# TensorE operands at chosen positions within a 64-byte line of SBUF, in a two-layer decoder trunk

## The chip, the cores and the metric

The kernel runs on one core of a Trainium2 chip. The metric is the device time of one execution in microseconds, lower is better.

## The reference

The input x has 256 positions of 1024 float32 values. Two layers follow each other; each is a token mixer and a feed-forward block, both on a root-mean-square norm of the running x and added to it.

- Layer 0's mixer is a short gated convolution: h times a 1024 x 3072 matrix gives three parts b, c and v; a causal convolution of width 3 over positions runs over c times v; the result times b goes through a 1024 x 1024 matrix.
- Layer 1's mixer is attention with 16 heads of 64 and rotary positions, causal over the 256 positions (one block, so the block selection selects nothing), with projections q, k, v and o.
- The feed-forward block of each layer goes up to 2 x 2816 columns, runs a causal width-3 convolution over positions, takes silu of one half times the other half, and goes down to 1024.

```python
x = x + short_conv_mixer(h, w_in, w_conv, w_out)      # layer 0
x = x + moba_attention(h, w_qkv, w_o)                 # layer 1
x = x + (silu(g) * u) @ w_down    # [g|u] = causal_dwconv(h @ w_up, w_conv), in both layers
```

A last norm gives the output.

## The kernel before

Everything is kept transposed, channels on the 128 partitions and positions along the free axis, so an activation tile is 128 x 256 float32. Each float32 operand of a product is split in two float32r tiles, a high part (the value rounded) and a low part (what is left). A product is then three matmuls, in `passes`: high weights with high inputs, high weights with low inputs, low weights with high inputs. Weights of 128 x 128 are the stationary operand and 256 columns of input the moving one, except in two places. In the v projection (`v_stage`) and in the down projection of layer 1 (`TokenAccum`) the inputs are stationary and 512 columns of weights move past them.

Weights are streamed in units of 128 x 1024 float32. A list made when the kernel is built, `PLAN`, has all units in the order of their use. `load_chunk` issues the DMAs of two units into a tile raw, four of which are in flight. `split_next` takes the next unit, makes its high tile hi on ScalarE and its low tile lo on VectorE, into rings of six tiles each. `unit(key)` hands out the pair and splits up to it if that has not been done. `slot` is called between groups of matmuls: it splits one or more units ahead and runs one step of each task that is waiting (evacuations, convolutions, softmax). The order on each engine is the order in which the code issues the instructions; the class `InOrder` pins it.

The stages of the program, in order, with the names that the profile's rows use:

- `FIRST`, the units of the first two column blocks of layer 0's input projection, in an order that follows x's arrival, and then "in", the rest of it. Outputs are cv and b, inputs xh and xl.
- "out", which sums up the mixer's output projection in PSUM over all its inputs (class `Accum`), between the "in" units. Output mo, inputs ys..h and ys..l.
- "up" and "down" of layer 0. Outputs gu and fo; inputs of up are xh and xl, of down ps_..h and ps_..l. Down is again an `Accum`.
- "q", "k" and "v" of layer 1 (outputs qk and v), the scores s, the transposes pt of the probabilities, the values o, and the output projection "o" (output ao, inputs oh and ol).
- "up" and "down" of layer 1, the latter a `TokenAccum`, and the last norm.

`scaled` makes xh and xl from x and the norm's gain; `split_tiles` gives the tiles for ys and ps; `values` those for oh and ol. `finish_norm` makes rms and rstd, each 260 columns wide. All instructions go through the call in `InOrder`, so the profile names line 92 for nearly all of them and rows are told apart by tile names.

Where a tile lies. SBUF tiles of a pool lie one behind the other, in the order of their first use, each beginning at a multiple of 32 bytes per partition. Three kinds of small tile are no multiple of 64 bytes long: eps and table (one column, 4 bytes, that take up 32), rms and rstd (1040 bytes, 1056 with the filling). Everything behind one of them is shifted by 32 bytes against a 64-byte line. The positions that come of this, as bytes past a multiple of 64:

| Stage (output) | Stationary operand | Moving operand |
|---|---|---|
| first, in (cv, b) | weights 32 | inputs 0 |
| out (mo) | weights 32 | inputs 32 |
| up of layer 0 (gu) | weights 32 | inputs 0 |
| down of layer 0 (fo) | weights 32 | inputs 32 |
| q, k (qk) | weights 32 | inputs 0 |
| v (v) | inputs 0 | weights 32 |
| o (ao) | weights 32 | inputs 32 |
| up of layer 1 (gu) | weights 32 | inputs 0 |
| down of layer 1 (fo) | inputs 32 | weights 32 |

A slice of a weight tile for one matmul begins at a multiple of 512 bytes in it, and a slice of an input at a multiple of 512 or 1024, so that every matmul of a stage has these positions. The transposes pt read both operands at 0.

Of the kernel before, what the change touches and what calls it, by code (L numbers as in the profile page):

```python
# [9 lines left out]
F32 = mybir.dt.float32  # L10
F32R = mybir.dt.float32r
# [3 lines left out]
P = 128  # L15
D = 1024
T = 256
# [7 lines left out]
U = 1024  # L25
# [5 lines left out]
SPLITS = 6  # L31
NBIG = 14
NT = 10
NPS = 7
WARM = 8

# [32 lines left out]
PLAN = weight_plan()  # L69
# [39 lines left out]
def trunk(ctx: ExitStack, tc: tile.TileContext, x, wall, small, ropes, masks, final, out):  # L109
# [5 lines left out]
    cp = ctx.enter_context(tc.tile_pool(name="cp", bufs=1))  # L115
    wp = ctx.enter_context(tc.tile_pool(name="wp", bufs=LOADS))
    ap_ = ctx.enter_context(tc.tile_pool(name="act", bufs=2))
# [9 lines left out]
    ones = cp.tile([P, P], F32, name="ones")  # L127
    ones_r = cp.tile([P, P], F32R, name="ones_r")

    def gain(i, m):  # L130
        return gn_c[:, i * ND + m : i * ND + m + 1]

# [10 lines left out]
    raw, hi, lo = {}, {}, {}  # L143
# [21 lines left out]
    def split_next():  # L165
        u = state["split"]
        if u >= NU:
            return
        state["split"] += 1
        c, o = CHUNK_OF[u]  # L170
        while state["dma"] <= min(c + LOADS - 1, len(CHUNKS) - 1):
            load_chunk()
        w = WIDTH[u]
        src = raw[c][:, o : o + w]
        hi[u] = wp.tile([P, w], F32R, name=f"hi{u}", tag="hi", bufs=SPLITS)
        lo[u] = wp.tile([P, w], F32R, name=f"lo{u}", tag="lo", bufs=SPLITS)
        if u < 2:
            V.tensor_copy(hi[u], src)
            if u == 0:
                scaled(0, (0,), nm0)  # L180
                split_next()
                for v, part in ((0, src), (1, raw[0][:, P : 3 * P])):
                    V.tensor_sub(lo[v], part, hi[v].bitcast(F32))
            return
        S.activation(hi[u], src, AF.Copy)
        V.tensor_sub(lo[u], src, hi[u].bitcast(F32))
# [55 lines left out]
    def scaled(i, ms, nm):  # L242

        for m in ms:
            xh = ap_.tile([P, T], F32R, name=f"xh{i}_{m}", tag=f"xh{m}", bufs=1)
            xl = ap_.tile([P, T], F32R, name=f"xl{i}_{m}", tag=f"xl{m}", bufs=1)
            S.activation(xh, xslice(m), AF.Copy, scale=gain(i, m))
            V.scalar_tensor_tensor(
                xl, xslice(m), gain(i, m), xh.bitcast(F32), op0=ALU.mult, op1=ALU.subtract
            )  # L250
            nm.xh[m], nm.xl[m] = xh, xl
# [12 lines left out]

    def table(func):

        t = ap_.tile([P, 1], F32, name="table", tag="table", bufs=1)
        S.activation(t, ones[:, 0:1], func)

    def finish_norm(i, nm, squared=False, cols=False, tag="b"):  # L270

        ps = bank(f"ss{i}", tag=tag)
        for part, total in enumerate(nm.total):
            kw = {"start": False, "stop": part == 1, "skip_group_check": True}
            E.matmul(ps[:, 0, :], ones_r, total, **{**kw, "start": part == 0})
            for t in range(2 if cols else 0):
                E.matmul(
                    ps[:, 1, 2 * t : 2 * t + 2], total[:, t * P : (t + 1) * P], ones_r[:, 0:2], **kw
                )
        n = T + 4 if cols else T  # L280
        rms = ap_.tile([P, T + 4], F32, name=f"rms{i}", tag="rms", bufs=1)
        ss = ps.rearrange("p a t -> p (a t)")[:, :n]
        S.activation(rms[:, :n], ss, AF.Sqrt, bias=eps, scale=1.0 / D)
        nm.r = ap_.tile([P, T + 4], F32, name=f"rstd{i}", tag="rstd", bufs=2)
        V.reciprocal(nm.r[:, :n], rms[:, :n])
        if squared:
            nm.r2 = ap_.tile([P, T], F32, name=f"rstd2{i}", tag="rstd2", bufs=1)
            V.tensor_mul(nm.r2, nm.r[:, :T], nm.r[:, :T])
# [131 lines left out]
    def pair_tile(name):  # L420
        return ap_.tile([P, 2, T], F32, name=name, tag="big", bufs=NBIG)

    def split_tiles(name):
        return tuple(
            ap_.tile([P, T], F32R, name=name + c, tag="ps" + c, bufs=NPS) for c in "hl"
        )

    def taps(y, src, w):
# [4 lines left out]


    V.memset(ones, 1.0)
    eps = cp.tile([P, 1], F32, name="eps")
    V.memset(eps, EPS)
    V.tensor_copy(ones_r, ones)
    o = NG * ND
# [20 lines left out]
    ys = {}  # L460
# [10 lines left out]
    def mix_b(j, b_ps, in_y, wait=1):  # L471
        for _ in range(wait):
            yield
        yb = half_tile(f"yb{j}")
        V.tensor_mul(yb, b_ps[:, 0, :], in_y[0])
        yield
        ys[j] = split_tiles(f"ys{j}")
        split_act(*ys[j], yb)

    firsts = [(bank(f"cv{j}", tag="a"), bank(f"b{j}", tag="a")) for j in range(2)]  # L480
    sums = sum_squares(0, nm, True)
# [47 lines left out]
    nm = Norm()  # L529
# [6 lines left out]
    def ffn(layer, nm, i, then):  # L536
        acc, ps = (TokenAccum if then is None else Accum)(f"fo{layer}"), {}
        gus = {}

        def whole(j):  # L540
            gn, y = pair_tile(f"gn{layer}_{j}"), pair_tile(f"gy{layer}_{j}")
            s, p = half_tile(f"s{layer}_{j}"), half_tile(f"p{layer}_{j}")
            V.tensor_mul(gn, gus[j], nm.r[:, None, :T].to_broadcast([P, 2, T]))
            yield
            for h in range(2):
                taps(y[:, h, :], gn[:, h, :], lambda t: ffn_tap(layer, t, h, j))
            yield
            S.activation(s, y[:, 0, :], AF.Silu)
            V.tensor_mul(p, s, y[:, 1, :])
            yield  # L550
            ps[j] = split_tiles(f"ps{layer}_{j}")
            split_act(*ps[j], p)

        for j in range(NF):
            if layer == 0 and j == 2:
                Q.dma_start(rope, ropes)
                Q.dma_start(mk, masks)
            gu = gus[j] = bank(f"gu{layer}_{j}")
            wg, wu = unit(("up", layer, 0, j)), unit(("up", layer, 1, j))
            if j == 0:  # L560
                for ks in ((0, 1), (2, 3), (4, 5), (6, 7)):
                    project(gu[:, 0, :], wg, nm, ks)
                    project(gu[:, 1, :], wu, nm, ks, start=False)
                slot()
                slot()
            else:
                project(gu[:, 0, :], wg, nm)
                slot()
                project(gu[:, 1, :], wu, nm, start=False)
                if j == 1:  # L570
                    finish_norm(i, nm)
                    table(AF.Silu)
                    spawn(whole(0))
                spawn(whole(j))
                slot()
            if j >= LAG_FFN:
                acc.add(("down", layer, j - LAG_FFN), ps[j - LAG_FFN], j == LAG_FFN, False)
                slot()
        for j in range(NF - LAG_FFN, NF - 2):
            acc.add(("down", layer, j), ps[j], False, False)  # L580
            slot()
        while tasks:
            slot(0)
        table(AF.Sqrt)
        acc.finish(
            [("down", layer, j) for j in (NF - 2, NF - 1)],
            [ps[j] for j in (NF - 2, NF - 1)],
            then,
        )
# [8 lines left out]
    nm = nm2  # L598
# [80 lines left out]
    def softmax(g, ps):  # L679
        sm = [pair_tile(f"sm{g}_{h}").rearrange("p a t -> p (a t)") for h in range(4)]  # L680
        mx, nmx, sums, inv = (
            ap_.tile([P, 8], F32, name=f"{n}{g}", tag=n) for n in ("mx", "nmx", "sums", "inv")
        )
        parts = [(2 * h + t, h, slice(c0, c1)) for h in range(4) for c0, c1, t in SPANS]
        for c, h, cols in parts:
            V.tensor_tensor_reduce(
                sm[h][:, cols], ps[h][:, cols], causal1 if c % 2 else causal0,
                op0=ALU.add, op1=ALU.max, scale=1.0, scalar=NEG, accum_out=mx[:, c : c + 1],
            )
            if c % 4 == 2:  # L690
                two = slice(2 * h - 2, 2 * h + 2)
                V.tensor_scalar(nmx[:, two], mx[:, two], -(HD**-0.5), None, op0=ALU.mult)
        yield
        for c, h, cols in parts:
            v = sm[h][:, cols]
            S.activation(
                v, v, AF.Exp, bias=nmx[:, c : c + 1], scale=HD**-0.5, accum_out=sums[:, c : c + 1]
            )
        if g == 0:
            yield  # L700
        V.reciprocal(inv, sums)
        for c, h, cols in parts:
            v = sm[h][:, cols]
            V.tensor_scalar(v, v, inv[:, c : c + 1], None, op0=ALU.mult)
        probs[g] = sm
# [13 lines left out]
    def values(g, now=False):  # L719
        pt = pts.pop(g)  # L720
        o = bank(f"o{g}")
        for e in range(2):
            for t in range(2):
                for h in (2 * e, 2 * e + 1):
# [5 lines left out]
                        stop=t == 1,  # L730
                        skip_group_check=True,
                    )
        hl = [ap_.tile([P, 2, T], F32R, name=f"o{c}{g}", tag=f"o{c}{g}", bufs=1) for c in "hl"]
        for e in range(2):
            os_[2 * g + e] = tuple(v[:, e, :] for v in hl)

# [47 lines left out]
    nm = Norm()  # L784
    for pair in range(4):
        ps = bank(f"ao{pair}")
# [102 lines left out]
```

## Time and profile before

| What | Value |
|---|---|
| Median of 3 runs | 585.46 us (585.14 to 585.8) |
| The profiled execution | 585.35 us |
| Its span, first to last instruction | 583.6 us |
| Instructions | 11250, of them 4628 matmuls |
| Busy TensorE, VectorE, ScalarE | 576.9, 464.1, 337.9 us |

[...] How fast TensorE works is read from the spacing of starts: the length of a run of matmuls back to back, over their count.

### The profile page before, as it was taken

To read this page: it belongs to the slowest core of one execution; us is meant where nothing else is said; L and a number is where in the kernel's file an instruction comes from. 1 tells how busy PE (TensorE), PEld (TensorE's weight loads), DVE (VectorE), ACT (ScalarE), POOL (GpSimd) and SP (SyncE) were. 2 spreads that over 40 slices of the span, in tenths; PEclk is the share of its full clock that TensorE was granted. 3 is DMA by queue.
4 is the path that set the end of the run, shared out by engine and by line. 5 is a ranking of instruction groups with operands and counts; after the bars stand their busy time and mean duration, and the time that the engine had idled before them with its cause. 6 is when DMAs were issued, how large, how long until landed. Compare 5 with 4: busy or idle time off the path is not lost.

```text
span 583.6 us, 11250 instructions
## 1 busy us (share of the span) xinstructions
PE 576.9 (99%) x4628; PEld 556.8 (95%) x4628; DVE 464.1 (80%) x783; ACT 337.9 (58%) x556; POOL 11.3 (2%) x12
## 2 busy tenths in 40 slices
PE   9999999999999999999999999999999999999996
PEld 9999999999999999999989998999999999999984
DVE  6997667899978778777899887477999778877873
ACT  7655446567655545555756557655666545554643
POOL 0022120000000000000000000000000000000000
PEclk9999999999999999999999999999999999999999
DMA  8957452746755455565255344453466455465201
GB/s 302 371 205 271 162 195 94 258 145 229 266 165 208 156 207 175 186 217 179 92 199 189 140 145 145 144 211 122 174 223 240 161 206 179 184 216 189 102 2 72
DMA packets 17188, 106.86 MB, mean 183 GB/s; under 512 B 1904, under 2 KB 3056, under 8 KB 4976
## 3 DMA queue, kind: packets, MB, share of 16 engines
q1 hardware_dynamic: 16704, 105.60, 51.0%
q8 instruction: 36, 0.59, 0.4%
q10 hardware_dynamic: 432, 0.54, 0.3%
q14 instruction: 16, 0.13, 0.1%
HBM read 105.09 MB, written 1.05 MB: 182 GB/s over the span
## 4 chain that ended last, share of the span: by engine, by line
PE 99%; ACT 0%; DVE 0%; issue 0%
PE gu L92 42%; PE fo L92 22%; PE cv L92 8%; PE qk L92 8%; PE ao L92 4%; PE mo L92 4%; PE b L92 4%; PE v L92 4%; PE s L92 1%; PE o L92 1%; PE pt L92 1%; PE busy L92 1%; PE ss L92 0%; ACT of L92 0%; DVE of L92 0%; ACT sq L92 0%
## 5 line engine op out<-in xcount | busy, mean ns | idle before, releaser
L92 DVE TENSOR_TENSOR lo<-raw,hi 128x1024 fp32r<-128x1024 f32 (+3 forms) x201 | 238.7, 1195 | 12.0 <-ACT hi L92 11.6
L92 ACT ACTIVATE hi<-raw 128x1024 fp32r<-128x1024 f32 (+2 forms) x199 | 203.3, 1034 | 13.2 <-PE cv L92 5.2
L92 PE MATMUL gu<-xh,hi 128*128 128x256 f32 x704 | 196.6, 279 | 0.0
L92 PE MATMUL gu<-xl,hi 128*128 128x256 f32 x704 | 196.6, 279 | 0.0
L92 PE MATMUL gu<-xh,lo 128*128 128x256 f32 x704 | 196.6, 279 | 0.0
L92 PEld LDWEIGHTS gu<-xl,hi 128*128 128x128 f32 x704 | 132.3, 188 | 0.8
L92 PEld LDWEIGHTS gu<-xh,hi 128*128 128x128 f32 x704 | 132.3, 188 | 0.7
L92 PEld LDWEIGHTS gu<-xh,lo 128*128 128x128 f32 x704 | 132.3, 188 | 0.0
L92 ACT ACTIVATE gy<-gn,sm 128x256 f32<-128x256 f32 x88 | 39.9, 502 | 79.9 <-DVE gn L92 79.9
L92 DVE SCALAR_TENSOR_TENSOR gy<-gn,sm,gy 128x255 f32<-128x255 f32 (+1 forms) x176 | 80.8, 481 | 3.1
L92 DVE TENSOR_TENSOR gn<-gu,rstd 128x512 f32<-128x512 f32 x44 | 30.2, 689 | 51.2 <-PE gu L92 51.2
L92 PE MATMUL qk<-xh,hi 128*128 128x256 f32 x128 | 36.3, 284 | 0.0
L92 PE MATMUL qk<-xh,lo 128*128 128x256 f32 x128 | 35.7, 279 | 0.0
L92 PE MATMUL qk<-xl,hi 128*128 128x256 f32 x128 | 35.7, 279 | 0.0
L92 PE MATMUL cv<-xh,hi 128*128 128x256 f32 x128 | 33.5, 283 | 0.0
L92 PE MATMUL cv<-xl,hi 128*128 128x256 f32 x128 | 33.4, 282 | 0.0
L92 PE MATMUL cv<-xh,lo 128*128 128x256 f32 x128 | 33.3, 281 | 0.0
L92 ACT ACTIVATE s<-gy 128x256 f32<-128x256 f32 x44 | 18.4, 418 | 16.4 <-DVE gy L92 16.3
L92 PEld LDWEIGHTS qk<-xh,hi 128*128 128x128 f32 x128 | 24.1, 188 | 0.5 <-issue 0.3
L92 PEld LDWEIGHTS qk<-xl,hi 128*128 128x128 f32 x128 | 24.1, 188 | 0.0
L92 PEld LDWEIGHTS qk<-xh,lo 128*128 128x128 f32 x128 | 24.1, 188 | 0.0
L92 PEld LDWEIGHTS cv<-xh,hi 128*128 128x128 f32 x128 | 23.3, 190 | 0.2 <-ACT hi L92 0.2
(474 smaller groups left out, 1083.7 us busy)
## 6 DMA issues: line engine op xcount, KB each, us to landing
raw<-wall SPq DMA_DIRECT2D x95, 1024.0 KB, 4.8
raw<-wall SPq DMA_DIRECT2D x6, 384.0 KB, 6.6
xt<-x SPq DMA_DIRECT2D x3, 256.0 KB, 6.2
out<-of SPq DMA_DIRECT2D x3, 256.0 KB, 2.1
raw<-wall SPq DMA_DIRECT2D x3, 192.0 KB, 4.5
gain_row<-final SPq DMA_DIRECT2D x1, 512.0 KB, 5.8
rope<-ropes SPq DMA_DIRECT2D x1, 384.0 KB, 5.3
out<-of ACTq DMA_DIRECT2D x1, 256.0 KB, 2.5
```

What stands on the lines that cost most here:

```text
L92: r = f(*args, **kw)
```

## The change

Each TensorE operand gets a position of its own within a 64-byte line, by stage. `LINE` is 16 float32 values, 64 bytes. The new helper `line` allocates a tile that is `off` values longer, filled up to a multiple of 16, and returns the part that begins at `off`. The two tables give `off` for weights and for inputs, in float32 values (4 is 16 bytes). The small tiles eps, table, rms, rstd and those of the softmax go through `line` without an offset, and so fill up to 64 bytes. Nothing else is edited: the instructions, their order, their shapes and the DMAs are the same.

```diff
+LINE = 16
+WEIGHTS_AT = {"first": 4, "in": 4, "out": 0, "up0": 12, "down0": 8, "q": 12, "k": 12, "v": 0, "o": 1, "up1": 4, "down1": 0}
+INPUTS_AT = {0: 0, "out": 8, 1: 0, "down0": 0, 2: 4, "o": 0, 3: 12, "down1": 8}
...
+    def line(pool, w, off=0, dtype=F32, **kw):
+
+        return pool.tile([P, -(-(off + w) // LINE) * LINE], dtype, **kw)[:, off : off + w]
...
-        hi[u] = wp.tile([P, w], F32R, name=f"hi{u}", tag="hi", bufs=SPLITS)
-        lo[u] = wp.tile([P, w], F32R, name=f"lo{u}", tag="lo", bufs=SPLITS)
+        kind = PLAN[u][0] + (str(PLAN[u][1]) if PLAN[u][0] in ("up", "down") else "")
+        hi[u], lo[u] = (
+            line(wp, U, WEIGHTS_AT[kind], F32R, name=f"{n}{u}", tag=n, bufs=SPLITS)[:, :w]
+            for n in ("hi", "lo")
+        )
...
-            xh = ap_.tile([P, T], F32R, name=f"xh{i}_{m}", tag=f"xh{m}", bufs=1)
-            xl = ap_.tile([P, T], F32R, name=f"xl{i}_{m}", tag=f"xl{m}", bufs=1)
+            xh, xl = (
+                line(ap_, T, INPUTS_AT[i], F32R, name=f"x{c}{i}_{m}", tag=f"x{c}{m}", bufs=1)
+                for c in "hl"
+            )
...
-        t = ap_.tile([P, 1], F32, name="table", tag="table", bufs=1)
+        t = line(ap_, 1, name="table", tag="table", bufs=1)
...
-        rms = ap_.tile([P, T + 4], F32, name=f"rms{i}", tag="rms", bufs=1)
+        rms = line(ap_, T + 4, name=f"rms{i}", tag="rms", bufs=1)
...
-        nm.r = ap_.tile([P, T + 4], F32, name=f"rstd{i}", tag="rstd", bufs=2)
+        nm.r = line(ap_, T + 4, name=f"rstd{i}", tag="rstd", bufs=2)
...
-            ap_.tile([P, T], F32R, name=name + c, tag="ps" + c, bufs=NPS) for c in "hl"
+            line(ap_, T, INPUTS_AT[kind], F32R, name=name + c, tag="ps" + c, bufs=NPS) for c in "hl"
...
-    eps = cp.tile([P, 1], F32, name="eps")
+    eps = line(cp, 1, name="eps")
...
-            ap_.tile([P, 8], F32, name=f"{n}{g}", tag=n) for n in ("mx", "nmx", "sums", "inv")
+            line(ap_, 8, name=f"{n}{g}", tag=n) for n in ("mx", "nmx", "sums", "inv")
...
-        hl = [ap_.tile([P, 2, T], F32R, name=f"o{c}{g}", tag=f"o{c}{g}", bufs=1) for c in "hl"]
+        hl = [
+            line(ap_, 2 * T, INPUTS_AT["o"], F32R, name=f"o{c}{g}", tag=f"o{c}{g}", bufs=1)
+            .rearrange("p (a t) -> p a t", a=2)
+            for c in "hl"
+        ]
```

All tiles ahead of an operand are now multiples of 64 bytes long, so the tables are the positions. In bytes, stationary and moving operand: first and in 16 and 0; out 0 and 32; up of layer 0 48 and 0; down of layer 0 32 and 0; q and k 48 and 16; v 16 (inputs) and 0 (weights); o 4 and 0; up of layer 1 16 and 48; down of layer 1 32 (inputs) and 0 (weights).

## Rows read from the trace of the kernel before

**Rows 1.** The page: span, then busy us, share of span and count by engine.
```profile
span 583.6 us, 11250 instructions
PE 576.9 (99%) x4628; PEld 556.8 (95%) x4628; DVE 464.1 (80%) x783; ACT 337.9 (58%) x556; POOL 11.3 (2%) x12
```

**Rows 2.** The page: the chain that ended last, by engine and by line.
```profile
PE 99%; ACT 0%; DVE 0%; issue 0%
PE gu L92 42%; PE fo L92 22%; PE cv L92 8%; PE qk L92 8%; PE ao L92 4%; PE mo L92 4%; PE b L92 4%; PE v L92 4%; PE s L92 1%; PE o L92 1%; PE pt L92 1%; PE busy L92 1%; PE ss L92 0%; ACT of L92 0%; DVE of L92 0%; ACT sq L92 0%
```

**Rows 3.** Waits of TensorE: who waited for whom, us in total, times, longest.
```profile
PE busy L92 <- DVE eps L92: 1.1, 1, 1.1
```

**Rows 4.** The chain in order of time, merged: start us, length us, what, count.
```profile
22.95 5.66 PE cv L92 x48
...
42.76 5.60 PE cv L92 x48
...
84.90 11.39 PE mo L92 x96
96.29 11.21 PE gu L92 x96
...
133.02 2.84 PE fo L92 x24
...
268.17 14.24 PE fo L92 x120
...
294.30 11.20 PE v L92 x48
...
318.42 1.31 PE pt L92 x12
...
369.86 21.55 PE ao L92 x180
391.41 11.20 PE gu L92 x96
...
429.80 2.78 PE fo L92 x12
...
563.98 13.95 PE fo L92 x60
```

**Rows 5.** Stretches: length; busy us by engine; granted clock; DMA share; GB/s.
```profile
core 0: us, PE busy (x) PEld busy (x) DVE busy (x) ACT busy (x) POOL busy (x), PEclk, DMA share, GB/s
22.95:39.91 16.96, 16.96 (x146) 16.96 (x146) 16.65 (x25) 9.07 (x14) 3.17 (x3) 1.00 0.63 231
...
84.90:96.29 11.39, 11.39 (x98) 11.39 (x98) 6.70 (x12) 4.46 (x9) 1.59 (x1) 1.00 0.54 186
96.29:107.50 11.21, 11.21 (x99) 11.21 (x98) 10.93 (x17) 7.46 (x11) 0.00 (x0) 1.00 0.31 99
127.41:268.17 140.76, 140.76 (x1203) 140.76 (x1202) 114.20 (x178) 81.44 (x123) 0.00 (x0) 1.00 0.57 199
...
294.30:305.50 11.20, 11.20 (x52) 8.74 (x51) 11.10 (x13) 4.75 (x6) 0.00 (x0) 1.00 0.55 192
369.86:391.41 21.55, 21.55 (x182) 21.55 (x183) 14.85 (x18) 13.45 (x19) 0.00 (x0) 1.00 0.48 172
...
424.19:563.98 139.79, 139.79 (x1010) 131.48 (x1009) 112.72 (x174) 79.47 (x121) 0.00 (x0) 1.00 0.50 174
```

**Rows 6.** Matmuls by tiles: shapes, count, busy us, mean ns; one pass of three.
```profile
L92 PE MATMUL gu<-xh,hi 128*128 128x256 f32 x704 | 196.6, 279 | 0.0
...
L92 PE MATMUL qk<-xh,hi 128*128 128x256 f32 x128 | 36.3, 284 | 0.0
...
L92 PE MATMUL cv<-xh,hi 128*128 128x256 f32 x128 | 33.5, 283 | 0.0
...
L92 PE MATMUL b<-xh,hi 128*128 128x256 f32 x64 | 18.0, 281 | 0.0
...
L92 PE MATMUL v<-hi,xh 128*128 128x512 f32 x32 | 12.8, 401 | 0.0
```

**Rows 7.** VectorE by form: 512 columns written at 0 (qa) and at 32 bytes (ol).
```profile
L92 DVE TENSOR_TENSOR qa<-qk,rope 128x512 f32<-128x512 f32 x4 | 2.8, 688 | 0.0
L92 DVE TENSOR_TENSOR ol<-o,oh 128x512 fp32r<-128x512 f32 x4 | 2.8, 688 | 6.0 <-ACT oh L92 6.0
```

**Rows 8.** The page: DMA issues, KB each, median us from issue to landing.
```profile
raw<-wall SPq DMA_DIRECT2D x95, 1024.0 KB, 4.8
```

More of the change, by code (lines that the diff above doesn't have):

```diff
@@ L421, in pair_tile, with split_tiles @@
         return ap_.tile([P, 2, T], F32, name=name, tag="big", bufs=NBIG)
-    def split_tiles(name):
+    def split_tiles(name, kind):
         return tuple(
-            ap_.tile([P, T], F32R, name=name + c, tag="ps" + c, bufs=NPS) for c in "hl"
+            line(ap_, T, INPUTS_AT[kind], F32R, name=name + c, tag="ps" + c, bufs=NPS) for c in "hl"
         )
@@ L476, in mix_b @@
         yield
-        ys[j] = split_tiles(f"ys{j}")
+        ys[j] = split_tiles(f"ys{j}", "out")
         split_act(*ys[j], yb)
@@ L550, in whole @@
             yield
-            ps[j] = split_tiles(f"ps{layer}_{j}")
+            ps[j] = split_tiles(f"ps{layer}_{j}", f"down{layer}")
             split_act(*ps[j], p)
```

## The prediction

> **What bounds the kernel now.** I read the page's busy shares first: TensorE is busy for 576.9 of 583.6 us, its weight loads for 556.8, VectorE for 464.1, ScalarE for 337.9 [rows 1]. The chain that ended last says the same by time: 99% of it is TensorE, and the products named gu hold 42% and fo 22% [rows 2]. Then who made TensorE wait: one wait of 1.1 us before the eight warm-up products and nothing else [rows 3]. So no wait can be removed by this change, and no engine stands in front of TensorE; what is left is how far apart in time two neighbouring matmuls start. The chain in order of time gives that: each of its pieces is a run of matmuls back to back, and length over count is the spacing [rows 4].
>
> The reader is to see four numbers there. A run of 96 gu products, each 256 columns, takes 11.20 us: 116.7 ns each. The cv run of 48 at 42.76 us gives 116.7 too. 96 mo products take 11.39 us and 120 fo products of layer 0 take 14.24 us: 118.7 ns each, with the same shape of weights and input. 48 v products of 512 columns take 11.20 us, 233.3 ns each, and of the fo products of layer 1, also of 512 columns, 12 take 2.78 us, 231.7 ns each (60 at the end, with the norm's work between, 13.95 us). The transposes pt, which load 128 weight columns like the others but move only 128 columns, take 109.2 ns each (12 in 1.31 us). [...]
>
> **Which differences go with position.** By the table of positions above, gu, cv, b and qk read weights at 32 bytes and inputs at 0; mo, fo of layer 0 and ao read both at 32. That is the split between 116.7 and 118.7 ns. Another reason would be the order of writes: mo and fo change the output bank after every three products, gu after 24. The ao products decide: they are looped like gu, 24 into one half bank, but read both operands at 32 bytes, and 180 of them take 21.55 us, 119.7 ns each. So position, not the output's order, is the likelier cause, and some 2.0 ns a product hang on it. The 512-column products show another sign: both operands at 32 give 231.7 ns, the weights at 32 against inputs at 0 give 233.3. A pair half a line apart is the better one in one shape and the worse in the other. And position is not all: the cv run of 48 at 22.95 us has the positions of the later ones and takes 5.66 us, 117.9 ns each.
>
> [...]
>
> **The change part by part.** It adds no instruction, no wait, no DMA and moves no step: it makes tiles up to 64 bytes longer and starts operands elsewhere. So each term is a count of matmuls by a change of spacing. Counts are from the grouped instructions [rows 6]: gu 2112, so 1056 a layer; qk 384; cv 384 and b 192; v 96; and from the plan 8 x 24 = 192 each for mo and ao, 22 x 24 = 528 for fo of layer 0, 22 x 12 = 264 for fo of layer 1.
>
> 1. Out, down of layer 0 and o: 912 matmuls that now have both operands at 32 get weights and inputs apart: (0, 32), (32, 0) and (4, 0) bytes. The second is exactly the pair that gu has now, the first its mirror, the third is new. I give all three gu's 116.7 in place of 118.7: 912 x 1.99 ns = 1.82 us less. Ends: nothing (if their 2 ns come from elsewhere), and 109.2 ns as for the transposes, 912 x 9.5 = 8.7 us less.
> 2. In, up of layer 0, q and k, up of layer 1: 576 + 1056 + 384 + 1056 = 3072 matmuls go from (32, 0) to (16, 0), (48, 0), (48, 16) and (16, 48). No row has a pair a quarter of a line apart, nor any operand at 16 or 48. Best bound: the transposes' 109.2 ns, 7.5 x 3072 = 23.0 us less. Worst: the pair at 118.7, 2.0 x 3072 = 6.1 us more. Rows at the two known pairs lie at 115.8 (231.7 halved), 116.7, 117.9 and 118.7 ns for 256 columns; the present one is in the middle of these, so a gain and a loss are both open. I take the best of them, 115.8: every one of these matmuls leaves position 32, which is the weights' place in every row of 118.7. 0.84 x 3072 = 2.57 us less. This is the term of which I am least sure.
> 3. V: weights, here the moving operand, from 32 to 0, inputs from 0 to 16. I take 231.7 for 233.3: 96 x 1.67 = 0.16 us less. Ends: twice 109.2, 1.4 us less; twice 118.7, 0.4 us more.
> 4. Down of layer 1: moving weights from 32 to 0, inputs stay at 32. V, half a line apart, has 233.3; staying has 231.7. I take no change. Ends: 13.3 x 264 = 3.5 us less, and twice 118.7, 5.7 x 264 = 1.5 us more.
> 5. Small tiles (the norm's rms and rstd, table, eps, the softmax's maxima and sums): only their own end moves. Nothing reads them faster or slower, by the rows; what they do is make the positions above exact. Cost 0.
> 6. Writers and loads: ScalarE writes hi, xh and the rest, VectorE writes lo and xl, at the new positions, and the raw weights that the DMAs write start at 0 where they started at 32. VectorE's subtraction of 512 columns takes 688 ns into ol at 32 bytes, and 688 ns as the product into qa at 0 [rows 7], so 32 bytes cost it nothing. Were they dearer, the cover is VectorE's 114.2 busy us of 140.8 in the feed-forward of layer 0 [rows 5]: 19% free. Without cover stands only the short stretch from 22.95 to 39.91 us, where VectorE is busy for 16.65 of 16.96 us: 2% on its weights' subtractions there would reach TensorE as some 0.3 us. A load lands in 4.8 us [rows 8], with three more in flight, and TensorE waits for none. Cost 0.
>
> Sum: 1.82 + 2.57 + 0.16 = 4.55 us less. The profiled execution took 585.35 us, 1.75 more than its span; it becomes 580.80. The median of the runs is 0.11 above it: **580.9 us**, 0.8% less.
>
> **Rivals.**
> - *The moved pairs are bad ones.* The 3072 matmuls of part 2 land at a spacing like that of mo and fo, 118.7 ns. Place: the projections. For it: the mo, fo and ao rows show that position can cost 2 ns, and no row says that an untried pair is better than the present. Against it: none of the new pairs has both operands at one place in the line, as all rows of 118.7 have. Price 6.1 us, less the 1.82 of part 1: 589.8. It decides the sign from 1.82 / 3072 = 0.6 ns a product on.
> - *Only the three pairs that are equal today gain.* Apart is as good as apart, whatever the distance: part 1 gives 1.82, part 2 nothing, and down of layer 1 may lose 1.67 x 264 = 0.4 as v shows. 583.6 to 584.1. For it: gu and v, both half a line apart, agree per column (116.7 and half of 233.3).
> - *The positions do nothing.* The 2 ns come from the order of products in these loops, the change does not do what it says: 585.5. For it: at one pair of positions cv has 117.9 and 116.7. Against it: ao, looped as gu, is slow. [...]
> - *A much better pair.* If the 7.5 ns that gu has above the transposes are two streams in each other's way, a pair that keeps them apart gives back half of it or more. Half: 11.5 (part 2) + 5.2 (part 1: from 118.7 to 112.9) + 0.7 + 1.8 (v and down of layer 1) = 19.2 us, so 566.2; all of it would be 36.6 us, 548.9. Against it: v moves 512 columns for each weight load and has the same excess per column, so half the loads did not halve it; and the transposes move half the columns, so their 109.2 may never be within reach.
>
> **How the numbers follow.** My sum 0.36; only the equal pairs 0.27; nothing 0.13; bad pairs 0.12; much better 0.12. The range of 571 to 587 leaves out most of the last (0.10) and the dear part of the bad pairs (0.08), and takes in the equal pairs, no effect, and part 2 from 4.1 ns a product less to 1.1 ns more (with part 1 and v as summed). The bound for same is 0.2%, 1.17 us, about what a measurement of this kernel can tell from no change: same is 584.3 to 586.6. Faster: my sum 0.36, much better 0.12, equal pairs 0.19, nothing 0.01, together 0.68. Same: equal pairs 0.08, nothing 0.10, bad pairs 0.02, together 0.20. Slower: bad pairs 0.10, nothing 0.02, together 0.12.
>
> **What would show it.** In the chain in order of time, pieces of 24 fo products in layer 0 go from 2.84 or 2.85 to 2.80 us, the 96 mo from 11.39 to 11.20, the 180 ao from 21.55 to about 21.2; 96 gu from 11.20 to 11.12; 12 fo in layer 1 stay at 2.78. The count of matmuls stays 4628, the granted clock 1.00, and TensorE's only wait is the warm-up's. I am wrong if gu at (48, 0) or (16, 48) comes out above 117.3 ns, if mo and fo stay at 118.7 with their operands apart, or if VectorE's or ScalarE's spans grow enough that TensorE waits for lo or hi.

## The result, and the profile after

The change makes the kernel slower: 589.58 us (median of 4 runs, 589.1 to 589.63) against 585.46, a ratio of 1.0068 with a 95% interval of 1.0051 to 1.0086. The forecast was 580.9. The profiled execution took 589.6 us, its span 587.8.

The page of the kernel after: span and busy time by engine, then the stages' pieces of the chain in order of time (start us, length us, what, count), as in [rows 4].

```profile
span 587.8 us, 11250 instructions
PE 580.9 (99%) x4628; PEld 560.7 (95%) x4628; DVE 463.9 (79%) x783; ACT 338.3 (58%) x556; POOL 11.3 (2%) x12
```

```profile
23.19 5.69 PE cv L97 x48
...
43.14 5.73 PE cv L97 x48
...
85.92 11.40 PE mo L97 x96
97.31 11.35 PE gu L97 x96
...
128.76 5.64 PE gu L97 x48
134.40 2.86 PE fo L97 x24
137.26 5.70 PE gu L97 x48
142.96 2.85 PE fo L97 x24
145.81 5.64 PE gu L97 x48
...
270.59 14.18 PE fo L97 x120
...
296.87 11.16 PE v L97 x48
...
372.79 21.48 PE ao L97 x180
394.27 11.34 PE gu L97 x96
...
568.25 13.94 PE fo L97 x60
```

The instructions are the same in number, VectorE and ScalarE are as busy as in [rows 1], and TensorE's waits, a list of who waited for whom (us in total, times, longest), are two:

```profile
PE busy L97 <- DVE eps L97: 1.1, 1, 1.1
PE cv L97 <- ACT hi L97: 0.3, 1, 0.3
```

So, but for that 0.3 us, the 4.2 us are neither work nor waiting: they are wider spacing. (The chains of E7 and E8 below, as this one, begin at a cv piece behind hi, of 0.50 us for two products, and nothing is lost there.) The granted clock was 0.997 to 1.00 in the four executions, and their times do not follow it: 589.1 us at 0.997, 589.63 at 1.00. By the starts of the pieces here and in [rows 4], the time up to the first gu grew by 1.02 us (96.29 to 97.31), the feed-forward of layer 0 by 1.34 (186.12 to 187.46), the attention by 0.50 and the feed-forward of layer 1 by 1.40. 96 gu products take 11.35 us, 118.2 ns each, where they took 116.7; cv 119.4 (5.73 over 48) where it had 116.7; fo of layer 0 118.2 where the forecast had 116.7. And gu now alternates, 5.64, 5.70, 5.64 us for 48, though its places in the line never change within a layer. Before, every such piece had 5.60 or 5.61. Three weight units go through rings of six slots for each pair of gu halves, so that every second pair uses the same slots.

### The profile page after: what moved, and what is told of

The parts are those of the page before. It is cut to its first block, busy times and chain, and to the rows that moved or that the text cites. A ratio compares the mean times of both kernels' runs of the same rounds, so it can differ in the third digit from the quotient of the medians.

```text
span 587.8 us, 11250 instructions
## 1 busy us (share of the span) xinstructions
PE 580.9 (99%) x4628; PEld 560.7 (95%) x4628; DVE 463.9 (79%) x783; ACT 338.3 (58%) x556; POOL 11.3 (2%) x12
## 4 chain that ended last, share of the span: by engine, by line
PE 98%; DMA 1%; ACT 0%; SPq 0%; DVE 0%; issue 0%
PE gu L97 42%; PE fo L97 21%; PE qk L97 8%; PE cv L97 8%; PE ao L97 4%; PE mo L97 4%; PE v L97 4%; PE b L97 4%; PE s L97 1%; PE o L97 1%; PE pt L97 1%; DMA raw<-wall 1%; PE ss L97 0%; SPq L97 0%; ACT of L97 0%; DVE of L97 0%
```

## The experiments

**First, slots against places.** The change fills each weight slot from 4096 to 4160 bytes and most input tiles from 1024 to 1088. Theory A blames that, theory B the new places within the line. Four kernels, beside the kernel before on one chip (585.36 us). E1 sets both tables to 0:

```diff
-WEIGHTS_AT = {"first": 4, "in": 4, "out": 0, "up0": 12, ...
+WEIGHTS_AT = {"first": 0, "in": 0, "out": 0, "up0": 0, ...
-INPUTS_AT = {0: 0, "out": 8, 1: 0, "down0": 0, 2: 4, "o": 0, 3: 12, "down1": 8}
+INPUTS_AT = {0: 0, "out": 0, 1: 0, "down0": 0, 2: 0, "o": 0, 3: 0, "down1": 0}
```

> The change with every entry of both tables at 0: slots are 4096 and 1024 bytes apart again, all operands begin at a 64-byte line. Theory A (uneven slots: the change makes ring slots 4160 and input tiles 1088 bytes apart, so that neighbouring matmuls no longer repeat one arrangement of addresses, and that costs some 1.4 ns a matmul; the position within 64 bytes matters little): gu has one spacing in all slots, at one of the two regular values, 116.7 or 118.7 ns, so 583 to 592 us. Theory B (positions: the new pairs within a line are worse, slots do not matter): both operands at one place in the line, as mo and fo had before, so all 256-column stages at 118.7 ns and 585.4 + 3072 x 2.0 ns = 591.5 us.

Measured: 588.52 us, ratio 1.0053 (1.0038 to 1.0068). Gu has 117.8 ns in every unit, but mo, fo of layer 0 and ao have 120.0 or 120.1, with both operands at 0 everywhere, and qk leaves its 117.8 once (72 products from 328.37 us on take 8.36 us, the 72 from 343.85 on 8.68). One place, more than one spacing: theory B as I had it is out. Nor is 117.8 one of theory A's two values, and even slots alone do not make a good kernel either.

E2 is the kernel before with longer weight slots and nothing else (the line for lo is left out here):

```diff
-        hi[u] = wp.tile([P, w], F32R, name=f"hi{u}", tag="hi", bufs=SPLITS)
+        hi[u] = wp.tile([P, U + 16], F32R, name=f"hi{u}", tag="hi", bufs=SPLITS)[:, :w]
```

> The kernel before with the weight rings' slots 64 bytes longer (4160 for 4096) and nothing else: every operand keeps its place within a 64-byte line. Theory A: about 589 us, gu near 118.2 ns and different from slot to slot. Theory B: as before, 585.4 us, gu at 116.7 ns in every slot.

Measured: 589.43 us, ratio 1.0069 (1.0054 to 1.0084), the whole loss of the change with no operand at another place in its line. Two of its gu pieces with the fo between, in the chain in order of time (118.8 and 119.2 ns a gu product):

```profile
127.87 5.70 PE gu L92 x48
133.57 2.84 PE fo L92 x24
136.41 5.72 PE gu L92 x48
```

E3 has the change's weight table, inputs at 0, and slots of 4608 bytes; E4 is the same with slots of 4160:

```diff
-            line(wp, U, WEIGHTS_AT[kind], F32R, name=f"{n}{u}", tag=n, bufs=SPLITS)[:, :w]
+            wp.tile([P, U + 128], F32R, name=f"{n}{u}", tag=n, bufs=SPLITS)[
+                :, WEIGHTS_AT[kind] : WEIGHTS_AT[kind] + w]      # E4: U + 16
```

> The weights at the change's positions, but slots 4608 bytes apart (a multiple of 512), inputs all at 0 in tiles of 1024: the positions within a line without the uneven slots. Theory A: gu of layer 0, at 48 and 0 bytes, has one spacing in all slots, near 116.7 ns; 583 to 587 us. Theory B: gu of layer 0 at 118.1 ns as in the change; 588 to 590 us.

> As the run before, with slots 4160 bytes apart as in the change: only the distance of the slots differs. Theory A: 588 to 590 us, gu near 118.2 ns and different from slot to slot. Theory B: the same as the run before within 0.3%.

Measured: E3 586.61 us, ratio 1.0021 (1.0012 to 1.0031); E4 589.59, ratio 1.0071 (1.0055 to 1.0088). The same places differ by 3.0 us by the distance of the slots alone, as theory A has it. Within E3, cv at (16, 0) has 116.7 ns in every unit, but gu of layer 0 at (48, 0) changes between 117.4 and 119.8 from pair to pair, against theory A's 116.7.

**Second, distance.** If even slots have one spacing a stage, what sets it? These runs move all activations on by whole lines, so that no place in a line changes, with the same edit in four sizes (24, 40, 72 and 136 columns give 64, 128, 256 and 512 bytes):

```diff
-        t = ap_.tile([P, 1], F32, name="table", tag="table", bufs=1)
+        t = ap_.tile([P, 24], F32, name="table", tag="table", bufs=1)[:, :1]
```

> The kernel before with all activations (xh, xl, ys, ps, oh and the rest) moved on by 64 bytes, so that each operand keeps its place within a 64-byte line and all slots keep their distances. Theory C (with even slots a stage's spacing is set by the distance between the two operands' addresses over more than a line): gu leaves 116.7 ns and mo and fo leave 118.7 by 0.5 ns or more, each to one value for the whole stage; total 582 to 591 us. Rival D (the place within the 64-byte line sets the spacing, and uneven slots alone spoil it): every stage as before, 585.4 us.

> As the run with 64 bytes, with 128. Theory C: mo and fo of layer 0, now 256 bytes past a multiple of 512 from their weights, take the 120.1 ns that they had at that distance with both operands at 0 in the line; total 582 to 592 us. Rival D: every stage as before, 585.4 us.

> As the run with 64 bytes, with 256. Theory C: mo and fo of layer 0 take the distance that ao had, 384, and so 118.7 ns; ao takes theirs, 128, and 118.6; gu at 288 is new and leaves 116.7. Rival D: every stage as before, 585.4 us.

> As the run with 64 bytes, with 512. Theory C, if the distance counts modulo 512: every stage as before, 585.4 us; if over more than that, some stage moves by 0.5 ns. Rival D: every stage as before, 585.4 us.

Measured, one execution each: 590.23, 589.02, 585.15 and 585.52 us; the kernel before beside them 585.21. Pieces of the chain in order of time, first 64 bytes on:

```profile
85.97 10.90 PE mo L92 x96
96.88 11.51 PE gu L92 x96
...
270.16 13.62 PE fo L92 x120
...
372.45 21.40 PE ao L92 x180
```

then 128 bytes on:

```profile
85.84 11.50 PE mo L92 x96
97.34 11.27 PE gu L92 x96
...
270.35 14.39 PE fo L92 x120
...
372.51 21.79 PE ao L92 x180
```

and 256 bytes on:

```profile
84.60 11.39 PE mo L92 x96
95.99 11.31 PE gu L92 x96
...
267.97 14.24 PE fo L92 x120
...
369.66 21.55 PE ao L92 x180
391.21 11.20 PE gu L92 x96
```

With 64 bytes gu goes from 116.7 to 119.9 ns and mo from 118.7 to 113.5; with 128, mo takes E1's 120 at another place in the line (11.50 over 96 is 119.8); with 512 these pieces have their old lengths of [rows 4] (11.39, 11.21, 14.24 and 21.55 us). With 256 they have them too, but for the first 96 gu (11.31 us, 117.8 ns; the next 144 are at 116.7 again) and one cv piece (5.65 us for 48). In these runs the spacings come back after 256 bytes (585.15 us for 585.21), not after 64 or 128 (590.23 and 589.02), and not only after 512 as Theory C had it for E7. Rival D falls by E5 and E6.

That makes the distance from weights to inputs, modulo 256, the number to look at. Before, gu had 32 and mo, fo of layer 0 and ao had 128. The change's slots, 16 x 256 + 64 bytes apart, and its input tiles, 4 x 256 + 64, mix four distances 64 bytes apart in every stage.

**Third, that distance put to use.** E9 is the change with its tables, operand tiles filled to 256 bytes (and NT = 9 for room). E10 is the kernel before with distance 192. E11 and E12 try 176 and 208, with weight slots of 4352 bytes and weights 16 bytes on.

```diff
+ROW = 64
...
-        return pool.tile([P, -(-(off + w) // LINE) * LINE], dtype, **kw)[:, off : off + w]
+        to = ROW if dtype == F32R else LINE                                          # E9
+        return pool.tile([P, -(-(off + w) // to) * to], dtype, **kw)[:, off : off + w]
...
+        t = ap_.tile([P, 48], F32, name="table", tag="table", bufs=1)[:, :1]         # E10
...
+            nm.r2 = ap_.tile([P, T + 40], F32, name=f"rstd2{i}", ...)[:, :T]         # E10
...
+            ap_.tile([P, 8 + (n == "mx") * 12], F32, name=f"{n}{g}", tag=n)[:, :8]   # E10
```

> The change with both tables as they are, but weight and input tiles filled up to 256 bytes where the change fills to 64 (and nine buffers of half tiles for ten, to make room). Every operand has the change's place in its 64-byte line; each stage now has one distance between its operands, counted modulo 256. Theory E (the spacing is set by that distance): one spacing a stage, 119.6 ns for gu of layer 0 at distance 16, 120.0 for gu of layer 1 at 96, 116.7 for cv and b at 48 and for qk and mo at 32, 118.1 for fo of layer 0 at 224; total about 591.8 us, above the change. Rival F (uneven slots alone cost, any even arrangement is as good as before): 585 to 586 us.

> The kernel before with small tiles made longer so that the distance from weights to inputs, modulo 256, is 192 in all stages but o (64 there); slots keep their distances. Both operands are at 32 in the line in every stage. Theory E: gu, cv, b and qk take mo's 114.2 ns, mo and fo of layer 0 too, v and fo of layer 1 about 229 ns per 512 columns; total about 573 us; should gu take the 117.8 that ao had at this distance, 584.5. Rival D (place within the line): all 256-column stages at 118.7, 591 us.

> Weights 16 bytes on, slots 4352 bytes apart (17 x 256), distance 176 for gu, cv, b and qk, 208 for mo and fo of layer 0. Theory E: one spacing a stage, between the 117.4 ns at 160, the 114.2 at 192 and the 118.1 at 224; total 572 to 586 us. Rival D gives no reason for less than 116.7 ns: 585 us or more.

> As the run before with the two distances exchanged: 208 for gu, cv, b and qk, 176 for mo, fo of layer 0 and ao. Theory E: gu here as mo in the run before and the reverse, within 1 ns; total 572 to 586 us. Rival D: 585 us or more.

Measured: E9 590.34 us, ratio 1.0088 (1.0074 to 1.0102). Theory E's spacings came for cv (116.7), gu of layer 1 (120.0), fo of layer 0 (118.2) and mo (116.7), and missed for qk (118.4 for 116.7). Gu of layer 0 has not the one value of 119.6: it changes between 117.5 and 119.8 from pair to pair, as in E3 at the same distance.

```profile
127.03 5.64 PE gu L98 x48
...
135.50 5.75 PE gu L98 x48
```

Rival F falls: even tiles at the change's places are no better than the change.

E10 575.14 us, ratio 0.9845 (0.9814 to 0.9875), its four runs 575.0 to 579.37. In its chain in order of time gu of layer 0 does what no row before did:

```profile
96.17 11.31 PE gu L92 x96
...
107.72 16.33 PE gu L92 x144
124.05 2.72 PE fo L92 x24
...
262.77 13.60 PE fo L92 x120
...
363.33 21.40 PE ao L92 x180
384.74 11.31 PE gu L92 x96
...
554.01 13.75 PE fo L92 x60
```

11.31 over 96 is 117.8 ns; 16.33 over 144 is 113.4, at the same distance and places. Between the two stand the two products of the norm's sums (ss), at 107.48 us. The theory's 573 us supposed 113 to 114 ns from the start.

E11 590.19 and E12 593.45 us (one execution each), both outside Theory E's total; Rival D's "585 us or more" fits them, but E5, E6 and E10 had ruled it out. Theory E's claim on the exchange held in layer 0: at 176 gu had 118.7 (E11), and mo, fo and ao 118.7 or 118.8 (E12); at 208 mo had 118.3, fo 117.8 (E11) and gu of layer 0 117.8 (E12). But the values were no interpolation of their neighbours, and gu of layer 1 in E12 ran at 123.1 for most units (5.91 us for 48), though gu of layer 0 had 117.8 at the same distance.

**Fourth, what else counts.** E13 moves everything behind eps on by 32 bytes, so that the distances of E10 stay in these stages and all operands begin at a line. (The ss products' own distance changes by 32 bytes, since their weights, `ones_r`, lie ahead of eps.) E14 lengthens xh, xl, ys and ps by 64 bytes in the kernel before, the other half of the change's filling.

```diff
+    eps = cp.tile([P, 16], F32, name="eps")[:, :1]                                   # E13
...
+            xh = ap_.tile([P, T + 16], F32R, name=f"xh{i}_{m}", ...)[:, :T]          # E14
```

> The kernel with distance 192, with everything behind eps moved on by 32 bytes: all distances stay, both operands of every stage now begin at a 64-byte line. Theory E (distance alone): each stage at 113.3 or 117.8 ns for 256 columns as in the run with distance 192, total 573 to 580 us. Rival D (the place within the line counts beside it): some stage at a spacing other than these two by 1 ns or more.

> The kernel before with xh, xl, ys and ps tiles 64 bytes longer, weights' slots as before: places within a line are those of before, distances of inputs and weights take four values in each stage. Theory E: gu, mo and fo near 118.2 ns, no even rhythm, total about 589 us, as with the weights' slots alone. Rival D: as before, 585.3 us.

Measured: E13 582.88 us, ratio 0.996 (0.9946 to 0.9974): above its range. Behind the first stage (113.3 ns) and up to the attention every stage ran at 117.8 ns, and gu of layer 1 at 117.8 and then at 113.3 with units of 114.4, as in E10. So Theory E's two values came, but gu and fo of layer 0 took 117.8 where E10 had 113.3. E14 589.69 us in one execution, beside 585.33, as expected: gu 119.0 ns (17.13 us for 144).

E15 to E18 interrupt E10 with further ss products, n of them, whose result the next product overwrites:

```diff
+        for _ in range(n):        # E15: 1 at norms 0 and 2; E16: 2 there; E17: 2 at 0, 1 at 1; E18: 2 at 0 and 1
+            E.matmul(ps[:, 0, :], ones_r, nm.total[0], start=True, stop=True, skip_group_check=True)
```

> The kernel with distance 192 with one more product of the norm's sums (its result is overwritten by the next) ahead of those of the first mixer and of the attention. Theory G (at one distance two rhythms keep themselves up; which one runs is handed on until an interruption changes it): cv, b, mo or qk at 113.3 in place of 117.8 ns, or still at 117.8, and nothing between; if both switch, total 570 us, if none 575.5. Against it: any third spacing of a whole stage.

> As the run before with two more products at each of the two places. Theory G: again 113.3 or 117.8 ns and nothing between, for whole runs of products, not necessarily the same as with one; total 570 to 580 us.

> The kernel with distance 192, two more products of the norm's sums at the first mixer and one more at the feed-forward of layer 0, none at the attention. Theory G: cv, b and mo at 113.3 ns as in the run with two more, gu and fo of layer 0 at 113.3 or 117.8 and nothing between; total 571.5 us if at 113.3, 579 if at 117.8.

> As the run before with two more at the feed-forward of layer 0. Theory G: the same two totals, 571.5 or 579 us, not necessarily the same one.

Measured: E15 575.53 us in one execution, cv, b, mo and qk as in E10. E16 579.12, also one: cv, b and mo at 113.3, then 117.8 from the ss products on. Its chain:

```profile
82.62 10.88 PE mo L92 x96
93.50 10.88 PE gu L92 x96
104.38 0.24 PE ss L92 x2
104.62 16.96 PE gu L92 x144
```

E17's profiled execution, of 572.91 us, from the first stage on, where a cv piece and the b product behind it are three products:

```profile
20.65 0.23 PE cv L92 x2
...
22.35 0.23 PE cv L92 x2
...
83.35 10.88 PE mo L92 x96
94.23 10.88 PE gu L92 x96
105.12 0.36 PE ss L92 x3
105.47 16.32 PE gu L92 x144
```

E18's, of 582.79 us:

```profile
20.55 0.24 PE cv L92 x2
...
22.32 0.24 PE cv L92 x2
...
85.33 11.31 PE mo L92 x96
96.64 11.31 PE gu L92 x96
107.94 0.47 PE ss L92 x4
108.42 16.96 PE gu L92 x144
```

10.88 over 96 and 16.32 over 144 are 113.3 ns; 11.31 and 16.96 are 117.8. No whole run of 256-column products before the attention had a third spacing. But one program has two times: E17's four executions took 572.91, 582.48, 582.34 and 571.68 us, E18's 582.79, 571.8, 582.64 and 572.35, at a granted clock of 0.998 or 0.999 in all eight. Theory G's 579 us did not come, and cv, b and mo were not at 113.3 in E18's profile. There all 2352 products of cv, b, mo, gu and fo in layer 0 have the wider spacing; 2352 times the 4.45 ns between the two is 10.5 us, and 582.8 less that is 572.3, the other pair of times.

The wider spacing is there before any ss product: 15 products of the first stage, between the first two lines shown, take 1.77 us in E18 (118.0 ns each) and 1.70 in E17 (113.3). E10, E13 and E16 start at 113.3 too, E15 at 117.8. From there on the ss products act alike in the five profiles, E10 and E15 to E18, leaving out the longer set of the attention: a pair of them changed the rhythm nine times of nine, three or four left it as it was six times of six. E10's run of 579.37 us fits this: with the first stage at 117.8, 144 products would be wider, the 720 up to the next pair narrower and 1560 behind it wider, 4.4 us in all by the 4.45 ns, so 579.5 for 575.1 (an estimate; that run has no profile). In E13, where the ss products have another distance, a pair changed the rhythm only the first of three times. So Theory G stands as to the two rhythms; what sets the one of the first stage is open.

Spacings of all runs with even slots, for 256-column products in ns (medians over units of 24, start to start; places are weights and inputs in bytes):

| Distance mod 256 | Places, spacing and run |
|---|---|
| 0 | (0, 0) 120.1 E1, 119.8 E3; (32, 32) 119.7 and 120.0 E6 |
| 16 | (48, 0) 117.4 to 120 E3, E9 |
| 32 | (32, 0) 116.7 and in single runs 117.8 before, E7, E8; (0, 32) 116.7 E9; (48, 16) 118.4 E9 |
| 48 | (16, 0) 116.7 E3, E9 |
| 64 | (0, 0) 117.8 E1, 113.3 for two units of its qk; (32, 32) 117.8 E10 |
| 80 | (48, 0) 118.1 E11 |
| 96 | (32, 0) 120.0 E5; (16, 48) 120.0 E9 |
| 128 | (32, 32) 118.6 before, E7, E8 |
| 160 | (32, 0) 117.3 and 118.6 E6 |
| 176 | (48, 32) 118.7 E11, E12 |
| 192 | (32, 32) 113.3 and 117.8 E10, E15 to E18, 114.2 and 117.8 E5; (0, 0) 113.3 and 117.8 E13 |
| 208 | (48, 0) 117.8 and 118.3 E11; 117.8, 118.3 and 123.1 E12 |
| 224 | (32, 0) 118.2 E3, E9 |
| 252 | (4, 0) 118.3 E3, E9 |

At 0, 64, 96 and 192 the usual spacing at two places in the line is the same. At 32 one of three, qk of E9, differs; whether by place or by rhythm is open. At 16, 32, 64, 160, 192 and 208 one distance and one pair of places have two spacings, so the distance does not settle the spacing alone.

## Why the prediction was wrong

The step that failed stands in the first sentence of the part by part: that the change makes tiles up to 64 bytes longer was given no price, and the place within 64 bytes was taken for all that matters. The longer slots alone bring the loss: E2 shows the whole of it (589.43 us) with the places of before, E14 too (589.69) from the inputs' side. What they change is the distance between weights and inputs. Even slots at the change's places (E9, 590.34) lose as much, with gu at distances 16 and 96. By the table, gu of layer 1 after the change, with 32, 96, 160 and 224 in equal parts, would have some 118.2 ns (an estimate, the mean of 116.7, 120.0, 118.0 and 118.2); it has 118.0. Two of the signs of being wrong came: gu above 117.3, and mo at 118.7 with its operands apart.

1. Out, down of layer 0 and o: 118.7 to 116.7 was forecast; mo stays at 118.7 (11.40 over 96), fo goes to 118.2, ao to 119.3. Moving operands apart within the line was no cure, because 32 and 128 modulo 256 were the difference between gu and mo, not (32, 0) and (32, 32). E5 shows it, where no operand leaves its place in the line and gu goes to 119.9, mo to 113.5; and so do E1 and E6: distance 0 is at 120 with both at 0 and with both at 32.
2. In, both ups, q and k: 0.84 ns less was taken, for leaving position 32; the first 96 gu of a layer, at 118.1 or 118.2, are 1.4 to 1.5 ns more, and 3072 x 1.4 is 4.3 us, the loss. The argument that 32 is "the weights' place in every row of 118.7" read a chance of the layout as a cause. The 115.8 was a rate of another stage's distance.
3. V: 232.5 ns (11.16 over 48) for 231.7 taken. Right within 0.1 us.
4. Down of layer 1: 13.94 us for 60, before 13.95. Right.
5. Small tiles at cost 0: right for what they do themselves, but their lengths set distances, as E5 and E6 show with a longer table: 5.0 and 3.8 us lost.
6. Writers and loads at no cost: right but for 0.3 us at most. TensorE's waits are the warm-up's and one of 0.3 us.

The rival of bad pairs gave 589.8, within 0.3 us of the result, but that was luck: E2 has the old pairs and the same loss. Its price of 2.0 ns a product was near the 1.4 that mixed distances cost. The rival of a much better pair had its place too: 113.3 ns was measured at distance 192 for gu, fo, cv and mo (E17); but it is not tied to one place within the line, since cv had it with both operands at 32 (E17) and with both at 0 (E13). That a pair keeps two streams out of each other's way, as that rival supposed, no run shows.

The line of 64 bytes was an assumption, and no run shows that SBUF has lines of that length: in E5 the inputs move by 64 bytes, every place within the line stays, and gu goes from 116.7 to 119.9 ns. Nor do the runs show which part of the chip makes the period of 256 bytes that E5 to E8 have (590.23, 589.02, 585.15 and 585.52 us).

## What to carry to other kernels

When TensorE is the bound and its matmuls run back to back, compare the spacing of starts between stages of one shape: in these runs one and the same product took 113.3 to 123.1 ns, and in E10 TensorE's only wait was the warm-up's 1.1 us. Keep the slots of a ring at a multiple of 256 bytes, so that each stage has one distance between weights and inputs, then try the distances by lengthening one tile ahead, and run each version several times, since distance 192 had two rhythms here (E17: 571.68 and 582.48 us), and the first stage's was handed on (E15 to E18). Here that gave 575.14 us (575.0 to 579.37) for three longer tiles, against 585.3; other distances (E11, E12) lost 4.9 and 8.2 us.

## What the runs showed of the hardware that was not expected

- In these runs the spacing of float32r matmuls of 256 columns went with the distance of the two operands' addresses modulo 256 bytes, though not with it alone: 113.3 to 123.1 ns, both ends at a granted clock of 0.997 (E10 and E12). Moving the inputs by 256 or 512 bytes left the total at 585.15 and 585.52 us for 585.21 (E7, E8); moving them by 64 changed a stage by up to 5.2 ns (E5, fo of layer 0, 118.7 to 113.5).
- At distance 192 two rhythms, 113.3 and 117.8 ns, each went on for over 170 us (E10 from 107.72 to 284.53 us, E16 from 104.62 to 288.35), and a pair of ss products between them changed one into the other nine times of nine in E10 and E15 to E18 (three or four did not, six times of six). Executions of one program differ by 10.8 us (E17, 571.68 and 582.48); all of layer 0 in the one rhythm for the other, as in the profiles of E17 and E18, is worth 10.5.
- With distances that change within a stage gu's mean lay at 118.2 to 119.0 ns (after, E2, E4, E14: 11.35, 11.38, 11.37 and 11.42 us for 96), inside the spread of the even ones.
- For 512 moving columns of weights past 128 of inputs the spacing also moved, from 226.7 ns (fo of layer 1 in E3, 2.72 us for 12) to 234.2 (v in E5, 11.24 us for 48).
